# Second-level Strassen sums 416 bytes lower in SBUF: a gap ahead of a tile pool is taken out

## The chip, the cores and the metric

The kernel runs on one core of one Trainium2 chip. The metric is the device time of one launch in microseconds. It is taken as the median of several runs; one further execution is recorded by the hardware profiler, and all views of the profile are of that one.

## The reference

The reference is one layer (`DEPTH = 1`) of a gated short-convolution mixer between two RMS norms, in float32, on 1,024 positions of 1,024 channels, with an inner width of 2,048:

```python
def short_conv_mixer(u, w_in, conv_w, w_out):
    z, bg, cg, v = jnp.split(u @ w_in.astype(u.dtype), 4, axis=-1)
    y = bg * causal_dwconv(cg * v, conv_w) * jax.nn.silu(z)
    return y @ w_out.astype(u.dtype)

u = rms_norm(h, pre_norm[i])
h = h + rms_norm(short_conv_mixer(u, ...), post_norm[i])
```

So there are two matrix products, 1,024 × 1,024 × 8,192 at the input and 1,024 × 2,048 × 1,024 at the output, with a convolution of three taps over positions, a SiLU gate and two norms around them.

## The kernel before

**Products.** Each float32 operand is split into a high and a low part of type float32r, and a product is taken as low·high + high·low + high·high, three matmuls. On top of that the kernel uses Strassen's scheme in Winograd's form: a product of two-by-two blocks takes seven block products, called a, b, c, e, d, f and g, on sums of blocks. For columns from `DEEP = 2` on, the block products b, f and g are themselves taken by seven smaller ones (`a'` to `g'`): this is the second level.

**Operands.** The moving operand at the input is the normed and transposed x and its sums. A tile `u_a`, `u_b` ... `u_g` (128 × 2 × 4 × 512) holds the high and low part of one of them, and lies in one of seven slots of SBUF. The second level has sums of its own: for each of b, f and g, three (`c'`, `d'`, `g'`) in a high and a low part, 18 tiles of 128 × 2 × 256 with the names `ubch_deep` ... `ugdl_deep` and the tag `ub`. They are computed once (`deep_split`, from line 1375) and read to the end of the input product. The other smaller products (`a'`, `b'`, `e'`, `f'`) read parts of `u_b`, `u_f` and `u_g`. The stationary operand, the weights, is always a page: one of 32 buffers of 2,048 bytes per partition, loaded by DMA, summed, split and freed again and again.

**One product.** A first-level product (`product`, from line 837) is 12 matmuls with 512 moving columns (names `px`, `pv`, `py` in the profile with `wah`, `wal` and so on for weights). A second-level product (`deep_product`, from line 1432) is 6 matmuls with 256 moving columns:

```python
for k in range(KQ):                       # KQ = 2
    hi, lo = (h[:, off + k * P : off + (k + 1) * P] for h in deep_w[z, c, n])
    ...
    nc.tensor.matmul(ps, lo, uh, ...)
    nc.tensor.matmul(ps, hi, ul, ...)
    nc.tensor.matmul(ps, hi, uh, ...)
```

**Order.** TensorE's order is the list `slots`. For each pair p of weight blocks and column c = p // 2 it holds the first-level products, with the second-level ones in runs between them, as these lines give them (first letter the block product, second the smaller one):

```python
sub = {"e": "ba bb", "a": "bc be", "d": "fa fb"}                                     # even p
sub = {"c": "fc fe", "e": "bf ff bd fd", "d": "bg fg gb ga", "a": "gf gc ge"}        # odd p
```

and `gg gd` of the column before behind c of an even p. b is worked this way for columns 2 to 15, f for 2 to 14, g for 2 to 13. The other engines' work is recorded and put in order by a planner (`Plan.arrange`) with fixed costs and due times that know nothing of addresses. Nearly all instructions are issued from one line of a helper, 279, so the profile names them by their tiles.

**Placement.** Tile pools are stacked in SBUF in the order in which they are opened: constants, small tiles, the U slots in two pools, the 32 pages, and behind them one stretch that is used three times: by `head` (`xa`, half of x, while it is normed and transposed), then by `tmp` (`gpad`, 1,026 floats, the convolution's padded input; `cv`, 1,024 floats, its output; then the 18 `ub` tiles), and in the output stage by `p2` (`acc`, `jk`). Distances between pools are set by a table and a helper (lines 205 to 215):

```python
U_LAYOUT = (
    ((0,3,4,), 64),
    ((1,2,5,6,), 0),
)
def gap(ctx, tc, name, size):
    if size:
        ctx.enter_context(tc.tile_pool(name=name, bufs=1)).tile([128, size // 4], F32, tag=name, name=name)
```

The table is read as: slots 0, 3 and 4, then 64 bytes that nothing uses, then slots 1, 2, 5 and 6, then no gap; behind them the pages. `U_SLOTS` deals the slots out: `u_a` 5, `u_b` 4, `u_c` 2, `u_e` 6, `u_d` 1, `u_f` 3, and 0 for `xb` and later `u_g`. In the output stage both operands of a product come from U slots (`oA`, `oy`, `ox` and `oB`, `ou`), dealt from the same list. A third gap, of 416 bytes (line 1011), lies between the pages and the stretch that is used three times.

Of the kernel before, what the change touches and what calls it, by code (L numbers as in the profile page):

```python
# [211 lines left out]
# [4 lines that stand above are left out]
# [426 lines left out]
def kernel(  # L642
# [365 lines left out]

    mixed = ExitStack()
    head = ExitStack()  # L1010
    gap(ctx, tc, "room_tmp", 416)
    hp = plan.pool(head.enter_context(tc.tile_pool(name="head", bufs=1, reuse_waits="tile")), 1)

    xa = hp.tile([P, TH, D], F32, tag="xa", name="xa")
# [1079 lines left out]
```

## Time and profile before

| | |
|---|---|
| three runs | 771.37, 771.75, 772.41 us; median 771.75 |
| profiled execution | 771.06 us, span 769.3 us |
| granted TensorE clock | 0.998 |
| TensorE busy | 759.3 us (99%), 4,320 matmuls |
| VectorE, ScalarE, GpSimd busy | 679.9, 459.1, 464.3 us |
| moved by DMA | 130.11 MB |

The span runs from the first instruction of the program to the last; the rest of the execution's time lies around it. In the profile PE is TensorE, PEld its weight loads, DVE VectorE, ACT ScalarE, POOL GpSimd. A matmul's row names its output, then the moving operand, then the weights. The end of a matmul is modelled, so that neighbouring ones overlap in the records; their starts are measured.

### The profile page before, as it was taken

What the parts mean: (1) busy time and instruction counts of PE and PEld (TensorE: products, weight loads), DVE (VectorE), ACT (ScalarE), POOL (GpSimd) and SP (SyncE); (2) the same over time, 40 slices, a digit from 0 to 9 for tenths busy, and PEclk for the clock granted to TensorE, in tenths of its full rate; (3) what the DMA queues carried; (4) which work ended last, traced back from release to release, by engine and by line L of the source; (5) the groups of instructions that cost most, each with busy time, mean ns of one, the idle gap of its engine ahead of it and who ended that gap; (6) DMA issues with size and microseconds to landing.
All of it is one profiled execution on the core that took longest, in us unless ns stands there. A gap on an engine that the chain in (4) does not pass through costs nothing.

```text
span 769.3 us, 12814 instructions
## 1 busy us (share of the span) xinstructions
PE 759.3 (99%) x4320; PEld 666.1 (87%) x4320; DVE 679.9 (88%) x1022; ACT 459.1 (60%) x880; POOL 464.3 (60%) x416
## 2 busy tenths in 40 slices
PE   8999999999999999999999999999999999999996
PEld 7888889898989898988898998989888889889885
DVE  6899978999888989999989999799998898877993
ACT  7765678675656565556555665556653656565731
POOL 2509997889675778696789678585639100700421
PEclk9999999999999999999999999999999999999999
DMA  9212425344333547566858484927465998566842
GB/s 316 69 53 71 123 79 150 105 128 141 100 117 97 171 111 198 137 177 174 239 138 240 110 234 107 251 84 217 127 174 177 332 373 289 199 220 205 276 149 109
DMA packets 117137, 130.11 MB, mean 169 GB/s; under 512 B 7320, under 2 KB 74704, under 8 KB 116944
## 3 DMA queue, kind: packets, MB, share of 16 engines
q1 hardware_dynamic: 112560, 120.77, 49.2%
q0 software_dynamic: 4352, 8.39, 7.0%
q8 instruction: 34, 0.56, 0.3%
q14 instruction: 31, 0.25, 0.1%
q10 hardware_dynamic: 160, 0.14, 0.1%
HBM read 101.74 MB, written 44.30 MB: 190 GB/s over the span
## 4 chain that ended last, share of the span: by engine, by line
PE 98%; DVE 1%; DMA 0%; ACT 0%; POOL 0%; issue 0%; POOLq 0%; ACTq 0%
PE px L279 39%; PE pv L279 15%; PE po_x L279 11%; PE px2b L279 5%; PE px2f L279 4%; PE px2g L279 3%; PE pp L279 3%; PE po_v L279 3%; PE pv2b L279 3%; PE pv2f L279 2%; PE pf_x L279 1%; PE pb_x L279 1%; PE py2b L279 1%; PE py L279 1%; PE pv2g L279 1%; PE pb_v L279 1%
## 5 line engine op out<-in xcount | busy, mean ns | idle before, releaser
L279 PE MATMUL px<-u_c,wch 128*128 128x512 f32 x248 | 76.5, 389 | 0.0
L279 PE MATMUL px<-u_a,wah 128*128 128x512 f32 x248 | 76.4, 389 | 0.0
L279 PE MATMUL px<-u_d,wdh 128*128 128x512 f32 x248 | 76.4, 389 | 0.0
L279 PE MATMUL pv<-u_e,weh 128*128 128x512 f32 x248 | 76.4, 389 | 0.0
L279 ACT COPY beside<-raw 128x512 f32<-128x512 f32 x67 | 39.6, 591 | 31.9 <-DVE dwf2l L279 10.5
L279 DVE SCALAR_TENSOR_TENSOR cv<-gpad,cw,cv 128x1024 f32<-128x1024 f32 x32 | 51.7, 1615 | 2.9 <-ACT cv L279 2.6
L279 PEld LDWEIGHTS px<-u_c,wch 128*128 128x128 f32 x248 | 46.6, 188 | 8.8
L279 PEld LDWEIGHTS px<-u_a,wah 128*128 128x128 f32 x248 | 46.5, 188 | 8.7
L279 PEld LDWEIGHTS pv<-u_e,weh 128*128 128x128 f32 x248 | 46.6, 188 | 8.7
L279 PEld LDWEIGHTS px<-u_d,wdh 128*128 128x128 f32 x248 | 46.5, 188 | 8.6
L279 POOL TENSOR_TENSOR sf<-raw,sc 128x512 f32<-128x512 f32 x30 | 46.4, 1545 | 10.1 <-DVE sc L279 5.8
L279 PE MATMUL px<-u_d,wdl 128*128 128x512 f32 x124 | 48.4, 390 | 0.0
L279 PE MATMUL px<-u_a,wal 128*128 128x512 f32 x124 | 48.3, 390 | 0.0
L279 PE MATMUL px<-u_c,wcl 128*128 128x512 f32 x124 | 48.3, 389 | 0.0
L279 PE MATMUL pv<-u_e,wel 128*128 128x512 f32 x124 | 48.2, 389 | 0.0
L279 POOL TENSOR_TENSOR rs_post<-ve_post,minus_half 128x1 f32<-128x1 f32 x7 | 6.5, 942 | 67.6 <-DVE ve_post L279 67.6
L279 POOL TENSOR_TENSOR raw<-raw,raw 128x512 f32<-128x512 f32 x31 | 44.6, 1437 | 3.3 <-DVE se L279 1.9
L279 POOL TENSOR_TENSOR sc<-se,raw 128x512 f32<-128x512 f32 x25 | 35.1, 1404 | 18.5 <-PE px2b L279 7.9
L279 ACT COPY sna<-px 128x512 f32<-128x512 f32 x30 | 17.6, 585 | 45.5 <-PE px L279 45.5
L279 POOL TENSOR_TENSOR se<-raw,raw 128x512 f32<-128x512 f32 x22 | 33.0, 1500 | 16.7 <-DMA raw<-in_sc_w_in 11.1
L279 DVE TENSOR_TENSOR wcl<-sc,wch 128x512 fp32r<-128x512 f32 x31 | 31.6, 1018 | 3.5 <-ACT wch L279 3.5
L279 POOL TENSOR_TENSOR sne<-snc,sne 128x512 f32<-128x512 f32 x12 | 18.4, 1536 | 23.1 <-ACT snc L279 23.1
(486 smaller groups left out, 2643.5 us busy)
## 6 DMA issues: line engine op xcount, KB each, us to landing
raw<-in_sc_w_in SPq DMA_DIRECT2D x128, 256.0 KB, 4.3
y_d<-cv SPq DMA_DIRECT2D x16, 512.0 KB, 2.9
s_d<-s SPq DMA_DIRECT2D x32, 256.0 KB, 4.7
t_d<-in_sc_w_out POOLq DMA_DIRECT2D x16, 512.0 KB, 8.8
tb<-in_sc_w_out SPq DMA_DIRECT2D x16, 256.0 KB, 3.2
t_d<-in_sc_w_out SPq DMA_DIRECT2D x16, 256.0 KB, 4.7
t_d<-t_d SPq DMA_DIRECT2D x16, 256.0 KB, 4.5
s<-y_d SPq DMA_DIRECT2D x16, 256.0 KB, 4.5
```

Of the source, the lines that this page charges most:

```text
L279: getattr(engine, name)(*(self.plain(a) for a in args), **{k: self.plain(a) for k, a in kw.items()})
```

## The change

One line goes: the gap of 416 bytes ahead of the stretch that `head`, `tmp` and `p2` use. All tiles in that stretch come to lie 416 bytes lower. The U slots and the pages stay where they are, as do all instructions and their order.

```diff
     mixed = ExitStack()
     head = ExitStack()
-    gap(ctx, tc, "room_tmp", 416)
     hp = plan.pool(head.enter_context(tc.tile_pool(name="head", bufs=1, reuse_waits="tile")), 1)
```

The tiles of `tmp` are made by these lines, in this order:

```python
gpad = tmp.tile([P, TAPS - 1 + L], F32, tag="gpad", name="gpad")
cvs[c] = tmp.tile([P, L], F32, tag="cv", name=f"cv_{c}")
deep[z, i] = [tmp.tile([P, KQ, HH], F32R, tag="ub", name=f"u{z}{i[0]}{h}_deep", bufs=18) for h in "hl"]
```

## The prediction

> **What bounds the kernel now.** I read the page's busy times and its chain first, then a table by stretches, then the timeline of TensorE alone.
>
> ```profile
> span 769.3 us, 12814 instructions
> PE 759.3 (99%) x4320; PEld 666.1 (87%) x4320; DVE 679.9 (88%) x1022; ACT 459.1 (60%) x880; POOL 464.3 (60%) x416
> PE 98%; DVE 1%; DMA 0%; ACT 0%; POOL 0%; issue 0%; POOLq 0%; ACTq 0%
> ```
>
> TensorE carries 98% of the chain that ends last.
>
> ```profile
> core 0: us, PE busy (x) PEld busy (x) DVE busy (x) ACT busy (x) POOL busy (x), PEclk, DMA share, GB/s
> 100.00:640.00 540.00, 539.98 (x3183) 479.85 (x3182) 492.79 (x750) 326.00 (x632) 374.97 (x339) 1.00 0.58 168
> ```
>
> In the 540 us that hold nearly all second-level products TensorE stands still for 0.02 us at a granted clock of 1.00. So the time is the number of matmuls times the distance from one start to the next. The mean of a group doesn't give that distance: its ends are modelled and overlap. The timeline does, by subtracting starts. Twelve matmuls of one product lie between neighbouring rows here:
>
> ```profile
> start us, us, engine line op out<-in xcount [idle before <-releaser]
> 62.29 0.39 PE L279 MATMUL py<-u_b,wbl 128*128 128x512 f32 x1
> ...
> 65.09 0.39 PE L279 MATMUL px<-u_c,wcl 128*128 128x512 f32 x1
> ...
> 67.83 0.39 PE L279 MATMUL pv<-u_e,wel 128*128 128x512 f32 x1
> ...
> 70.55 0.39 PE L279 MATMUL px<-u_d,wdl 128*128 128x512 f32 x1
> ```
>
> With u_b a matmul takes 2.80/12 = 233.3 ns, with u_e 2.72/12 = 226.7 ns. Shape, clock and kind of weights are the same. What differs is the place in SBUF. All pages, and so all weights, have one residue r of their address modulo 512 (r = 128 in the program's allocation). U slots 1, 2, 5 and 6 (u_a, u_c, u_d, u_e) have r as well; slots 0, 3 and 4 (u_b, u_f, u_g) end 64 bytes earlier because of the 64-byte gap in `U_LAYOUT`. Call d the bytes by which weights lie past the moving operand modulo 512: d = 0 gives 226.7 ns and d = 64 gives 233.3 ns at 512 columns. Behind u_b, u_c takes 2.74 us for its twelve: a change of d costs a little once.
>
> For 256 columns, which is what the change touches, the output stage shows three values of d in runs of 24 matmuls, because there both operands come from U slots:
>
> ```profile
> 652.32 2.89 PE L279 MATMUL pb_x<-ox_b,oA_b 128*128 128x256 f32 x24
> 655.05 0.39 PE L279 MATMUL po_x<-ou_c,oy_c 128*128 128x512 f32 x1
> ...
> 701.56 2.99 PE L279 MATMUL pf_y<-oB_f,oA_f 128*128 128x256 f32 x24
> 704.39 2.99 PE L279 MATMUL pf_x<-oB_f,oA_f 128*128 128x256 f32 x24
> 707.22 3.03 PE L279 MATMUL pf_v<-oB_f,oA_f 128*128 128x256 f32 x24
> 710.08 3.03 PE L279 MATMUL pf_x<-oB_f,oA_f 128*128 128x256 f32 x24
> 712.95 2.90 PE L279 MATMUL pf_v<-oB_f,ox_f 128*128 128x256 f32 x24
> 715.69 0.75 PE L279 MATMUL pf_x<-ox_f,oA_f 128*128 128x256 f32 x5
> ```
>
> By the slots that `U_SLOTS` deals out, the row at 701.56 has d = 64: 2.83/24 = 117.9 ns. The one at 704.39 has d = 448: 2.83/24 = 117.9 ns. Those at 707.22 and 710.08 have d = 0: 119.2 and 119.6 ns. The rows at 652.32 and 712.95 have d = 64 again, behind d = 448 and d = 0: 2.73/24 = 113.8 and 2.74/24 = 114.2 ns. So d = 64 has two steady speeds, and what ran before decides which. The second-level sums themselves:
>
> ```profile
> 358.46 0.28 PE L279 MATMUL px<-uggh_deep,dwg 128*128 128x256 f32 x1
> ...
> 359.16 0.28 PE L279 MATMUL px2g<-ugdh_deep,dwg2l 128*128 128x256 f32 x1
> ...
> 359.87 0.39 PE L279 MATMUL pv<-u_e,wel 128*128 128x512 f32 x1
> ```
>
> Two products of six take 1.41 us: 117.5 ns each, the slower of the two speeds of d = 64.
>
> **The change, part by part.** It removes no instruction and adds none. Everything allocated behind the pages moves down by 416 bytes. Thirty-two pages of 2,048 bytes keep the residue r; the gap of 416, then `gpad` with 4,104 bytes rounded up to 4,128, then `cv` with 4,096 put the sums (tag `ub`) at r + 416 + 32 = r + 448, so d = 64. Without the gap they lie at r + 32, so d = 480. `gpad`, `cv`, `xa`, `acc` and `jk` move with them; pages and U slots stay.
>
> How many matmuls read the sums:
>
> ```profile
> L279 PE MATMUL px2b<-ubgh_deep,dwb 128*128 128x256 f32 x56 | 12.2, 281 | 0.0
> ...
> L279 PE MATMUL pv<-ufgh_deep,dwf 128*128 128x256 f32 x52 | 11.3, 281 | 0.0
> ...
> L279 PE MATMUL px<-uggh_deep,dwg 128*128 128x256 f32 x48 | 10.4, 281 | 0.0
> ```
>
> Four of a product's six matmuls read the high part, so 14, 13 and 12 columns are worked this way; with three sums each that is 39 × 3 × 6 = 702 matmuls.
>
> Their price at d = 480 is in no row. The lower bound is 113.8 ns, the best 256-column distance shown: (113.8 − 117.7) × 702 = −2.7 us, with 117.7 as the mean of 117.5 and 117.9. The upper one among these runs is 119.6 ns: +1.9 × 702 = +1.3 us. d = 480 lies 32 bytes from 0 and 32 from 448. I take d = 0, because moving tile and weights then begin in the same 64 bytes (128 to 191 modulo 512), which at d = 448 they don't: **+1.3 us**.
>
> Next, changing between values of d. Before, a run of second-level products (d = 64) and the next 512-column product (d = 0) follow each other without loss. From d = 0 at 256 columns into 512 columns the trace shows this:
>
> ```profile
> 718.55 3.14 PE L279 MATMUL po_x<-ou_d,oy_d 128*128 128x512 f32 x13
> ```
>
> Steady, thirteen would span 12 × 0.2267 + 0.39 = 3.11 us, so the passage costs 0.03 us. Runs that end in sums come after each odd e (`bd fd`, 14 times) and each even c (`gg gd`, 12 times): 26 × 0.03 = **+0.8 us**, with 0 as the lower bound.
>
> Third, the products of u_b, u_f and u_g that follow sums in one run: `fe`, `gb ga`, `ge`, `be`, 13 + 24 + 12 + 14 = 63 products. Their d stays 64, but they may fall into the fast speed, as behind d = 0 at 712.95. Where all did, 378 × (113.8 − 117.9) = −1.5 us, less the passage back. But only six or twelve matmuls follow, and the first ones pay: in the run at 712.95 the first passage is in the mean of 114.2. I take **−0.2 us**, between −1.5 and 0.
>
> The other tiles that move:
>
> ```profile
> L279 DVE SCALAR_TENSOR_TENSOR cv<-gpad,cw,cv 128x1024 f32<-128x1024 f32 x32 | 51.7, 1615 | 2.9 <-ACT cv L279 2.6
> ...
> L279 PE MATMUL pk<-ident,xa 128*128 128x128 f32 x32 | 4.9, 279 | 1.6 <-DVE ve_pre L279 1.2 <-DVE xa L279 0.4
> ...
> L279 PE MATMUL pk<-ident,xb 128*128 128x128 f32 x32 | 4.1, 272 | 0.0
> ```
>
> The convolution on `gpad` and `cv` runs on VectorE beside TensorE, which waited 0.02 us in 540; I cost it at nothing. Without that cover, 3% of 51.7 us would be 1.6 us. The transposes out of `xa` (32 of them) take 0.8 us longer in all than those out of `xb`, mostly before the first of them; between −0.8 and +0.8 I take 0. `acc` at the end: 0, with the same cover except in the last store. The DMAs keep their sizes and order, and no queue is changed.
>
> Sum: 1.3 + 0.8 − 0.2 = **+1.9 us**. The profiled execution took 771.06 us (span 769.3 and 1.8 around it) and would take 773.0. It is 0.7 us below the median of the three runs, 771.75, which becomes **773.7 us**.
>
> The Trainium skill speaks against any change. "SBUF — State Buffer", section "Who interferes with whom", says that "PE and ACT never wait on anyone", and "TensorE: Matmul & The Clock Gate", Part 2, that loading weights takes no SBUF read bandwidth from the running matmul. By that rule the sum is 0. The trace disagrees, with 233.3 against 226.7 ns for the same instruction at another address.
>
> **The rivals.** *Faster: the sums fall into the fast speed.* [...] It decides from the point where the distance in the rows of `ubch`, `ubdh` and `ubgh` is below 116 ns. Price: −2.7 us for the sums, −1.5 for the products behind them, and the passage back into 512 columns, for up to 78 runs (six per column, 13 columns). Behind the run at 652.32 the trace has it:
>
> ```profile
> 655.05 3.12 PE L279 MATMUL po_x<-ou_c,oy_c 128*128 128x512 f32 x13
> ```
>
> Against the steady 3.11 us that is 0.01 us, +0.8 in all: together −3.4 us, 768.4 us. For it: that speed exists. Against it: no run begins in it, and at d = 448 and d = 0, the neighbours on both sides, none of the 24 reaches it.
>
> *Slower by more: a start within 64 bytes costs a step.* The one step that the 512-column rows show is 233.3 − 226.7 = 6.6 ns per matmul. If the sums at r + 32 paid it each time, 702 × 6.6 = +4.6 us, 776.4 us. For it: no moving operand now starts off a multiple of 64. Against it: nothing shows it.
>
> *No change.* Either the rule above holds here, or d = 480 behaves as d = 448 does (117.9 ns) and passages cost nothing: 0 to +0.5 us, 771.8 to 772.3 us.
>
> **How the numbers follow.** The bound of 0.2% is 1.5 us, about what a measurement of this kernel can tell from no change. The forecast has 0.48; of it 0.12 stays within the bound, since each of its terms may be half as large. The large step has 0.14, no change 0.18, the fast speed 0.20. So slower 0.36 + 0.14 = 0.50, same 0.12 + 0.18 = 0.30, faster 0.20. The range must leave out no more than 0.2: about half of the fast case below and a third of the large step above, 769.0 to 776.6 us. The forecast alone, from 0 to the upper bounds (1.3 + 0.8 + 0.8), spans 771.8 to 774.7.
>
> **What would show it.** Right: twelve matmuls on sums take 1.43 us instead of 1.41; the first 512-column product behind `fd` or `gd` takes 2.75 us instead of 2.72; u_a, u_c, u_d and u_e stay at 2.72; TensorE's idle time in 100 to 640 us stays at nothing. Wrong: sums at 113 to 114 ns or at 124 ns; an unchanged 117.5; products of u_b behind sums that take under 0.69 us for six; or a new wait of TensorE, since an order made for one timing is now run at another.

## The result and the profile after

The changed kernel takes 773.2 us (median of 8 runs, 772.53 to 774.51) against 771.15 for the kernel before, run beside it (8 runs, 770.38 to 772.41). The ratio is 1.0028, with a 95% interval of 1.0017 to 1.0039. The profiled execution took 772.96 us, and its page begins so:

```profile
span 771.2 us, 12814 instructions
PE 761.6 (99%) x4320; PEld 665.8 (86%) x4320; DVE 677.6 (88%) x1022; ACT 459.0 (60%) x880; POOL 462.6 (60%) x416
```

The same 12,814 instructions have a span 1.9 us longer, and TensorE is busy 2.3 us longer. The stretch from 100 to 640 us, with the columns of before:

```profile
100.00:640.00 540.00, 539.89 (x3166) 477.13 (x3166) 488.01 (x745) 325.03 (x629) 374.48 (x339) 1.00 0.58 168
```

TensorE is still full (539.89 of 540 us) at a clock of 1.00, but starts 3,166 matmuls where it started 3,183. So the loss is in the distance between starts, as forecast, and not in a wait. Where in the order of products it lies is read from one run, `bg fg gb ga`, and the 512-column product behind it. Before:

```profile
348.07 0.28 PE L279 MATMUL px2b<-ubgh_deep,dwb 128*128 128x256 f32 x1
...
349.48 0.28 PE L279 MATMUL px<-u_g,dwg0l 128*128 128x256 f32 x1
...
350.90 0.39 PE L279 MATMUL px<-u_a,wal 128*128 128x512 f32 x1
...
353.62 0.28 PE L279 MATMUL px<-u_g,dwg2l 128*128 128x256 f32 x1
```

After:

```profile
349.08 0.28 PE L279 MATMUL px2b<-ubgh_deep,dwb 128*128 128x256 f32 x1
...
350.48 0.28 PE L279 MATMUL px<-u_g,dwg0l 128*128 128x256 f32 x1
...
351.90 0.39 PE L279 MATMUL px<-u_a,wal 128*128 128x512 f32 x1
...
354.66 0.28 PE L279 MATMUL px<-u_g,dwg2l 128*128 128x256 f32 x1
```

The two products on sums take 1.40 us instead of 1.41: they have become slightly faster. The two on u_g take 1.42 both times. The product on u_a, whose operands the change doesn't touch and which lies two products behind the last sum, takes 2.76 us instead of 2.72. Behind a run that ends in sums the loss is smaller:

```profile
359.54 0.28 PE L279 MATMUL px<-uggh_deep,dwg 128*128 128x256 f32 x1
...
360.94 0.39 PE L279 MATMUL pv<-u_e,wel 128*128 128x512 f32 x1
...
363.69 0.28 PE L279 MATMUL px2b<-u_b,dwb0l 128*128 128x256 f32 x1
```

Here 12 matmuls on sums take 1.40 us and the product on u_e 2.75.

Over the whole trace I took each product's time from its first start to the next product's, and the median of each kind; a few products with a single late start don't count in it. In nanoseconds per product (6 matmuls of 256 columns, 12 of 512; S is a product on sums, U one on u tiles):

| | before | after | products | difference in all, us |
|---|---|---|---|---|
| S | 707 | 702 (first of a run), 700 (behind S) | 117 | −0.6 |
| U behind S | 707 | 706 | 51 | 0.0 |
| 512 columns behind a run that ends in S | 2,720 | 2,744 | 27 | +0.6 |
| 512 columns behind a run with S that ends in U | 2,720 | 2,765 | 49 | +2.2 |
| 512 columns behind a run of U alone | 2,720 | 2,720 | 27 | 0.0 |

That adds up to +2.2 us, against 2.05 between the medians, whose interval of 1.0017 to 1.0039 is 1.3 to 3.0 us. The loss is paid by products whose own operands never moved.

### The profile page after: what moved, and what is told of

The parts are those of the page before. It is cut to its first block, busy times and chain, and to the rows that moved or that the text cites. A ratio compares the mean times of both kernels' runs of the same rounds, so it can differ in the third digit from the quotient of the medians.

```text
span 771.2 us, 12814 instructions
## 1 busy us (share of the span) xinstructions
PE 761.6 (99%) x4320; PEld 665.8 (86%) x4320; DVE 677.6 (88%) x1022; ACT 459.0 (60%) x880; POOL 462.6 (60%) x416
## 4 chain that ended last, share of the span: by engine, by line
PE 98%; DVE 1%; DMA 0%; ACT 0%; POOL 0%; issue 0%; POOLq 0%; ACTq 0%
PE px L279 39%; PE pv L279 15%; PE po_x L279 11%; PE px2b L279 5%; PE px2f L279 4%; PE px2g L279 3%; PE pp L279 3%; PE po_v L279 3%; PE pv2b L279 3%; PE pv2f L279 2%; PE pf_x L279 1%; PE pb_x L279 1%; PE py2b L279 1%; PE py L279 1%; PE pv2g L279 1%; PE pb_v L279 1%
```

## The experiments

The theory formed from these traces: the sums' own price at d = 480 is no loss; TensorE carries a state from one 256-column product to the next, d and the number of columns decide where it settles, and passing back to 512 columns costs what it takes to settle again. The rivals are named in each expectation.

**The sums alone back.** The gap stays out, and `cv`'s buffer is made longer:

```diff
-        cvs[c] = tmp.tile([P, L], F32, tag="cv", name=f"cv_{c}")
+        cvs[c] = tmp.tile([P, L + 104], F32, tag="cv", name=f"cv_{c}")[:, :L]
```

> The gap stays out, so gpad, cv, xa, acc and jk lie where the change put them, but cv's buffer is 416 bytes longer, which puts the sums alone back to d = 64. Theory (the time is lost where d goes from 480 to 64 or 0, none of it in the other tiles): about 771.2 us, ratio to the kernel before 0.999 to 1.001, twelve 512-column matmuls behind a run with sums back to 2.72 us from 2.74 to 2.77. Rival (the moved convolution and output tiles, or waits on them): stays near 773.2 us, ratio 1.002 to 1.004.

It took 770.91 us, ratio 0.9997 (0.9988 to 1.0006). The product behind the same run is back at 2.72 us:

```profile
350.79 0.39 PE L279 MATMUL px<-u_a,wal 128*128 128x512 f32 x1
...
353.51 0.28 PE L279 MATMUL px<-u_g,dwg2l 128*128 128x256 f32 x1
```

So the place of the sums makes the whole difference; that of `gpad`, `cv`, `xa` and `acc` makes none that shows.

**All of the second level at 480**, with the u tiles' gap at 480 as well:

```diff
-    ((0,3,4,), 64),
+    ((0,3,4,), 480),
```

> The change, and the U slots of u_b, u_f and u_g also to d = 480, so that every second-level product has the same d and no run changes it inside. Theory of the passages: the 45 ns behind runs that end in u products become the 24 ns seen behind runs that end in sums, but for all of some 104 runs (+2.5 us against before); 256-column matmuls on u tiles go from 117.8 to 116.7 ns (936 of them, -1.0 us), the sums keep -0.8 us; 512-column matmuls on u_b, u_f, u_g (225) between 226.7 and 233.3 ns, -1.5 to 0 us: 770.4 to 771.9 us in all. Rival (a 512-column product pays a fixed 45 ns once any run before it held d = 480): +4.7 us for the passages, 772.6 to 774.1 us.

It took 773.16 us, ratio 1.0028 (1.0018 to 1.0038): above the first theory's figure and within the rival's. The trace separates the two. The product on u_a behind the run that ends in u_g:

```profile
351.50 0.39 PE L279 MATMUL px<-u_a,wal 128*128 128x512 f32 x1
...
354.24 0.28 PE L279 MATMUL px<-u_g,dwg2l 128*128 128x256 f32 x1
```

It takes 2.74 us, as behind sums in the change, and so does, at the median, every kind of 512-column product with d = 0 behind a run; there is no 45 ns left. U products take 700 ns behind another product instead of 707. Their own tiles did not move in this run: the wider gap lies behind slots 0, 3 and 4 and moves the pages, and so the weights. So it is the distance between the two operands that counts, and not the address of the moving tile by itself. What the expectation left out is the output stage. There d = 448 became 32, and 64 became 480, because the slots' distance from each other grew. The 512-column matmuls at d = 32 take 233.3 ns in the mean against 229.0 before; in all the stage lost 1.2 us. Without that the kernel would be at about 772.0, by the upper end of the theory's range. The rival's fixed 45 ns falls.

**The whole input product at 480**: one pool of seven slots and a gap of 480 behind it. In the output stage, where both operands come from these slots, d is then 0 throughout.

```diff
-    ((0,3,4,), 64),
-    ((1,2,5,6,), 0),
+    ((0,3,4,1,2,5,6,), 480),
```

> The change, and all seven U slots at d = 480: in the input product d never changes. Theory of the passages: none is left, second-level matmuls take 116.7 ns throughout (1,638 of them, -1.8 us against before); what a 512-column matmul takes at d = 480 is in no run yet, and decides: at 226.7 ns 769.0 to 769.5 us, at 230 ns (a half step, as 116.7 is half a step above 113.3) about 776 us. Rival (d = 480 itself is costly wherever it stands): above 776 us.

It took 778.57 us, ratio 1.0098 (1.0085 to 1.0112): above both of the theory's figures, and where the rival puts it. The run and the product behind it:

```profile
352.46 0.28 PE L278 MATMUL px2b<-ubgh_deep,dwb 128*128 128x256 f32 x1
...
355.26 0.40 PE L278 MATMUL px<-u_a,wal 128*128 128x512 f32 x1
...
358.06 0.28 PE L278 MATMUL px<-u_g,dwg2l 128*128 128x256 f32 x1
```

Four products take 2.80 us, 116.7 ns a matmul, and no second-level product is more than 4 ns off 700 any more. No passage costs anything, as the theory has it: each 512-column product takes 2.80 us behind a run and elsewhere. But that is 233.3 ns a matmul, a whole step above 226.7, where the theory allowed half a step at most. So for 512 columns the rival is right, d = 480 is costly wherever it stands; for 256 columns it is not, 116.7 ns is less than the 117.8 of before.

**The sums at d = 0**: a gap of 480 in place of 416.

> The gap is 480 bytes instead of 416, which puts the sums at d = 0 and leaves the u tiles at 64 and 0. Theory of the passages: what counts is that d changes between the sums and the u tiles, so this kernel loses at least as much as the change: 51 runs at some 45 ns and 26 at some 30 ns, +3 us, and the sums at 118 to 120 ns another 0.2 to 1.5 us: 774 to 776 us. Rival (only a start off a multiple of 64 bytes upsets what follows): the passages cost nothing, the sums 0 to 1.5 us, 771.2 to 772.7 us.

It took 772.56 us, ratio 1.0021 (1.0012 to 1.0030): below the theory's figures, which took every passage to be as dear as in the change, and within the rival's. The rival falls by the trace all the same:

```profile
359.68 0.28 PE L279 MATMUL px<-uggh_deep,dwg 128*128 128x256 f32 x1
...
361.11 0.40 PE L279 MATMUL pv<-u_e,wel 128*128 128x512 f32 x1
...
361.81 0.40 PE L279 MATMUL pv<-u_e,wel 128*128 128x512 f32 x1
```

The first three matmuls on u_e take 0.70 us instead of 0.68 although everything starts at multiples of 64 bytes, and sums and u_e both have d = 0. So it isn't a change of d alone that costs: the passage from 256 to 512 columns costs at one and the same d. Over all runs the product behind sums takes 2,747 ns. A product on sums takes 713 ns as the first of a run, 720 as the second. And u products behind sums become faster: 699 ns, and 680, the fast speed, where a second one follows.

**Four more places of the sums**, each by the size of the gap: 224 bytes give d = 256, 352 give 128, 384 give 96 and 448 give 32.

```diff
-    gap(ctx, tc, "room_tmp", 416)
+    gap(ctx, tc, "room_tmp", 224)
```

> The gap is 224 bytes: the sums at d = 256, all else as before. Theory (the own price of d lies between 113.3 and 120 ns, and the passages add up to 45 ns wherever d changes by anything but 64 to 0): sums -3.1 to +1.5 us, passages +1.2 to +3.3 us against before: 769.3 to 776 us. Rival (passages cost only where an operand starts off a multiple of 64 bytes): no 512-column product behind a run takes over 2.72 us, 768.1 to 772.7 us.

> The gap is 352 bytes: the sums at d = 128, all else as before. Theory: as at d = 256, passages of 20 to 45 ns behind the runs with sums, 769.3 to 776 us. Rival (off multiples of 64 alone): passages free, 768.1 to 772.7 us.

> The gap is 384 bytes: the sums at d = 96, 32 bytes from the u tiles' 64 and off a multiple of 64. Theory: a change of d by only 32 shifts the passage less than 416 does: sums 116 to 119 ns, passages 0 to 24 ns, 770.0 to 773.0 us. Rival (off multiples of 64 alone): passages as in the change, 24 and 45 ns, 772.5 to 774 us.

> The gap is 448 bytes: the sums at d = 32, between the u tiles of the second level (64) and those of the first (0). Theory: sums between the 117.8 of d = 64 and the 119.4 of d = 0 or a half step below, 116.7 to 119; passages between the 0 of d = 64 and the 27 ns of d = 0: 770.4 to 772.7 us. Rival (off multiples of 64 alone): as the change, 773.2 us.

All four are slower than before, by times and by products (medians in ns; the S column has the first S of a run and one behind another S; the last two columns are the 512-column product, behind a run that ends in S and behind one with S that ends in U):

| d of the sums | us | ratio, 95% interval | S first, S behind S | U behind S | 512 columns behind S | 512 columns behind S, then U |
|---|---|---|---|---|---|---|
| 64 (before) | 771.15 | | 707, 707 | 707 | 2,720 | 2,720 |
| 480 (the change) | 773.2 | 1.0028 (1.0017 to 1.0039) | 702, 700 | 706 | 2,744 | 2,765 |
| 0 | 772.56 | 1.0021 (1.0012 to 1.0030) | 713, 720 | 699 | 2,747 | 2,735 |
| 32 | 773.34 | 1.0026 (1.0015 to 1.0038) | 710, 709 | 705 | 2,748 | 2,765 |
| 96 | 772.94 | 1.0023 (1.0012 to 1.0034) | 716, 710 | 706 | 2,734 | 2,765 |
| 128 | 772.88 | 1.0021 (1.0010 to 1.0032) | 716, 720 | 696 | 2,764 | 2,735 |
| 256 | 772.44 | 1.0017 (1.0006 to 1.0028) | 712, 720 | 699 | 2,748 | 2,735 |

The rival that only starts off a multiple of 64 bytes upset what follows falls at d = 128 and 256 by the products (at 256 the time, 772.44 us, lies in both ranges). It holds a part: behind u products, the three places off a multiple of 64 cost 45 ns at the median and the others 15; only in the runs `bg fg gb ga` do d = 96 and 32 cost less, 15 ns and nothing. At d = 96 and 32 the theory expected cheaper passages than the trace shows; at d = 32 its time, at most 772.7 us, missed too, and the rival's 773.2 was met. Of these seven places, only d = 64 leaves the next 512-column product at 2,720 ns everywhere.

**One sum at d = 0.** The last test of the carried state takes the kernel before and moves one of its nine sums, the one that opens the run `bg fg gb ga`:

```diff
+            if (z, i) == ("b", "g'"):
+                both = tmp.tile([P, 2 * KQ * HH + 16], F32R, tag="ubk", name="ubg_deep")
+                parts = (both[:, 16 + n * KQ * HH : 16 + (n + 1) * KQ * HH] for n in (0, 1))
+                deep[z, i] = [t.rearrange("p (k l) -> p k l", k=KQ) for t in parts]
...
-            deep[z, i] = [tmp.tile([P, KQ, HH], F32R, tag="ub", name=f"u{z}{i[0]}{h}_deep", bufs=18) for h in "hl"]
+                deep[z, i] = [tmp.tile([P, KQ, HH], F32R, tag="ub", name=f"u{z}{i[0]}{h}_deep", bufs=16) for h in "hl"]
```

> The kernel before, with one of the nine sums alone (b's g', which opens the run bg fg gb ga) at d = 0; all others stay at 64. Theory (a stretch of 256-column matmuls carries a state from one product to the next, and d only says where it settles): bg takes 713 ns, then fg 699, gb and ga 680 each instead of 707, and the 512-column product behind the run 2.735 us instead of 2.72: -41 ns for each of 13 runs, -0.5 us in all, about 770.6 us; 13 of the runs of ubg to u_g in the trace fall to 113.3 ns. Rival (each product has the price of its own d, whatever ran before): bg 720 ns, all others 707 and the next product 2.72 us: +0.2 us, 771.3 us.

```profile
347.74 0.88 PE L279 MATMUL px2b<-ubg_deep,dwb 128*128 128x256 f32 x6
348.45 0.29 PE L279 MATMUL pv<-ufgh_deep,dwf 128*128 128x256 f32 x1
...
349.15 0.28 PE L279 MATMUL px<-u_g,dwg0l 128*128 128x256 f32 x1
...
349.83 0.28 PE L279 MATMUL px2g<-u_g,dwg0l 128*128 128x256 f32 x1
...
350.51 0.39 PE L279 MATMUL px<-u_a,wal 128*128 128x512 f32 x1
...
353.24 0.28 PE L279 MATMUL px<-u_g,dwg2l 128*128 128x256 f32 x1
```

The products take 0.71, 0.70, 0.68 and 0.68 us, then 2.73. In all twelve complete runs of this kind they stand at 711 to 714, 698 to 700, 679 to 681 twice, and 2,734 to 2,736 ns: the run and the product behind it take 41 ns less than before. The products behind the first have the same shape and the same d as in the kernel before; only what ran ahead of them differs. The rival falls. In time it is too little to see: 771.01 us, ratio 0.9995 (0.9986 to 1.0004). It is the nearest to a better version that these runs gave, and not shown to be one.

The trace of the kernel before holds such a switch as well, without any change of address. Behind two matmuls that start about 0.1 us late each, at 416.83 and 417.05 us, the product on `ubd`, with d = 64 as ever, runs at the fast speed:

```profile
417.63 0.28 PE L279 MATMUL px2b<-ubdh_deep,dwb2l 128*128 128x256 f32 x1
...
418.31 0.28 PE L279 MATMUL px2f<-ufdh_deep,dwf2l 128*128 128x256 f32 x1
```

It takes 0.68 us instead of 0.71, and in the next experiment's trace, with two late starts at the same place, it does so again. A late start thus seems able to set what is carried too, and not addresses alone. It doesn't always: behind another one, at 407.6 us, the matmuls go on at 117.8 ns.

**The same sum at d = 448**, with 32 in place of 16 in the lines above.

> As the run before with that one sum at d = 448 instead of 0. Theory of a carried state: bg 707 ns, then fg 692 (as behind d = 448 in the output stage), gb and ga 680, and 2.735 us behind: -54 ns for each of 13 runs, -0.7 us, about 770.4 us. Rival (the price of its own d alone): 707 ns for all, 2.72 us behind, 771.1 us.

This missed. The run takes 0.71, 0.70, 0.71 and 0.71 us, and 2.72 behind it:

```profile
348.18 0.87 PE L279 MATMUL px2b<-ubg_deep,dwb 128*128 128x256 f32 x6
348.89 0.28 PE L279 MATMUL pv<-ufgh_deep,dwf 128*128 128x256 f32 x1
...
349.59 0.28 PE L279 MATMUL px<-u_g,dwg0l 128*128 128x256 f32 x1
...
351.01 0.39 PE L279 MATMUL px<-u_a,wal 128*128 128x512 f32 x1
...
353.73 0.28 PE L279 MATMUL px<-u_g,dwg2l 128*128 128x256 f32 x1
```

It took 771.36 us, ratio 1.0003 (0.9994 to 1.0012). In all twelve such runs the products lie within 5 ns of the rival's figures. That d = 448 led to the fast speed in the output stage does not carry over: there the matmuls ahead of it were others. So d of the product ahead isn't enough to say which state follows. What the state is made of was not measured.

## Why the prediction was right, and where it was not

The forecast was 773.7 us, +1.9 on the profiled execution; that came out as +1.9 (span 769.3 to 771.2), and the medians stand 2.05 apart. Its sum was right, and two of its three terms were wrong by about as much in opposite directions, −1.9 and +2.4 us. That the number came out so close is therefore luck in good part. Of its four signs of being right, two came: 2.744 us behind runs that end in sums, and a TensorE that stays full. The sums did not take longer, and the 512-column products did not all stay at 2.72 us.

- *What bounds the kernel, and that addresses set the distance of starts*: right. TensorE stayed full, and putting back the sums alone brought the time back.
- *The price of the sums, +1.3 us, by the row of d = 0*: wrong in sign. They take 116.7 ns behind other sums and 117.1 as the first of a run: −0.6 us. The choice between the two neighbours was mistaken: neither d = 0 (119.6 ns) nor d = 448 (117.9) stood for 480. The measured price lies inside the bounds, 113.8 and 119.6.
- *The passage behind runs that end in sums, 26 × 0.03 = +0.8 us*: right. 27 × 0.024 = +0.6 us (the run `bg fg` of column 14 ends in sums too).
- *U products behind sums, −0.2 us*: the step that failed most. Their own speed did not change, but the 512-column product behind them pays 45 ns, 49 times: +2.2 us. The step had taken the passage back from d = 64 as free because it was free before, where the run had also begun at d = 64.
- *The other moved tiles at nothing*: right for the time. Single late starts moved about, and the figure of TensorE's idle time doesn't hold them, since ends are modelled: one product of u_g at 557 us starts its second matmul late in the changed kernel and also with the sums alone put back, where the time is as before.
- *The rule of the Trainium skill* ("SBUF — State Buffer", section "Who interferes with whom", that TensorE never waits on anyone; "TensorE: Matmul & The Clock Gate", Part 2, that a weight load takes no read bandwidth of SBUF from the running matmul), taken as no change, would have left the time at 771.15 us. The traces disagree with that forecast: 226.7 to 233.3 ns for one instruction of 512 columns and 113.3 to 120 ns for one of 256, by addresses and by what ran before. That the reading of weights is what delays the moving operand is not shown by any run.
- *The rivals*: the fast speed did not come with the change, but it did come to u products behind sums at d = 0. The large step of 6.6 ns per matmul did not show at 256 columns; at 512 columns and d = 480 it did.

## What to carry to other kernels

Where TensorE is full, its distance from start to start is worth reading from the timeline by product and by what ran before, because the place of moving tile and weights modulo 512 was worth 3% of a matmul here at 512 columns and up to 6% at 256. The price of a new placement is to be looked for in the products behind the moved one too, and past the next change of shape: here the moved products gained 0.6 us and the 512-column products behind their runs lost 2.8. A steady speed read from one stage does not say that the same addresses give that speed in another.

## What the runs showed of the hardware that was not expected

- At the same d = 64, 256-column matmuls ran at 117.8 or at 113.3 ns, and one product of six matmuls ahead of them at another address switched between the two, in all twelve such runs.
- As the second product on sums in a run, 256-column matmuls took in the mean 116.7 ns with d = 480, 118.2 with 32, 118.3 with 96 and 120 with 0, 128 and 256; with 64 they ran at 117.8 or 113.3. 512-column matmuls take 226.7 ns with d = 0 and 233.3 with 64 and with 480. So d = 0 is the best place measured for 512 columns and among the worst for 256.
- Where the passage costs, a 512-column product with d = 0 loses 15 to 45 ns, spread over its first three to nine matmuls, before it is back at its steady speed. Two different passages can begin at the same speed: u products at 117.7 to 117.8 ns cost the next one nothing before the change and 45 ns after it.
